# RG-LRU gates as half-row float32 products, both gates of a head side by side

## The chip, the cores and the metric

One core of a Trainium2 chip runs the whole program. The metric is device time in microseconds, from the first to the last instruction and what lies around them; lower is better. TensorE (PE) multiplies 128x128 stationary tiles with up to 512 moving columns into PSUM banks, ScalarE (ACT) evaluates functions, VectorE (DVE) does elementwise work and scans, GpSimd (POOL) does little here, and SyncE (SP) issues most DMAs.

## The reference

Two layers of a backbone over 256 latent tokens with a prefix of 256 context tokens, width 1024. Each layer has a token mixer with two branches (RG-LRU and HGRN2) and a ConvFFN. The change lies in the RG-LRU gates. There are 16 heads of 64 channels; each head has its own 64x64 matrix for each gate and direction:

```python
def rglru_coeffs(x, wa, ba, wx, bx, lam):
    xh = x.reshape(B, L, RG_HEADS, RG_HEAD_DIM)
    r = jax.nn.sigmoid(jnp.einsum('blhi,hij->blhj', xh, wa).reshape(B, L, D_RG) + ba)
    i = jax.nn.sigmoid(jnp.einsum('blhi,hij->blhj', xh, wx).reshape(B, L, D_RG) + bx)
    log_a = -RG_C * jax.nn.softplus(-lam) * r
    a = jnp.exp(log_a)
    b = jnp.sqrt(-jnp.expm1(2.0 * log_a)) * (i * x)
```

A linear scan h = a h + b follows, forwards and backwards, over context and then latents.

## The kernel before

Activations lie feature-major: 128 channels (a tile `t`, two heads) on the partitions, 512 tokens (256 latents, 256 context) in the columns. The big products are split: each float32 operand becomes a high and a low part (type fp32r), and `mm3` adds three products of the parts. `piece` makes the parts of the weights, `whi` on ACT (L221) and `wlo` on DVE (L222), into three buffers each; a new piece waits until PE has used an old one.

`rg_phase` runs once a layer. `PAT` gives its order: X is a group of the input projection whose rows feed the recurrence, F a group of the other rows, R a recurrence of two tiles (`recur`). There are four recurrences a layer. `gate_w` loads the gate matrices of a tile: it clears `gwr` on GpSimd (L552) and brings the two 64x64 blocks of a gate onto the diagonal of a 128x128 matrix, by four DMAs on SP (L555), for two gates and two directions. In layer 0 ACT and DVE split these (`gwh`, `gwl`, L562 and L563), and the input `xc` too (`xs`, L573 and L574); in layer 1 (`exact`) the products are full float32 without a split (L580). Each gate product has its own PSUM bank from `aux()`, four banks that the tag `ax` shares with all side products, and is read by one sigmoid (L583, which the profile shows at the helper's line L79).

After the sigmoids of two tiles come exp and tanh, a sqrt, two products and four scans of 256 tokens for each tile on DVE (L591 to L607), and L609 adds the directions. `r` and `q` (the tile `i[t]`) have two buffers each, so the first write of a recurrence's `q` waits for L609 of the recurrence before. Functions keep their order through `act`; a change of function set loads a table (ACT_TABLE_LOAD).

A scheduler fixes the order of the instructions on each engine when the kernel is built, from priorities and its own estimates of durations. At run time every engine takes its instructions strictly in that order.

Of the kernel before, what the change touches and what calls it, by code (L numbers as in the profile page):

```python
# [14 lines left out]
P = 128  # L15
# [12 lines left out]
# schedule of the start: a = a part of the conditioning, l / c = rows of latents / context, w = weights of a group,  # L28
# n = a pair of feature tiles normed and modulated, m = its products, s / t = per-channel columns
ORDER = 'laacwanaaawanasmnmmnmt'  # L30
# order of the RG phase per layer: X = a group of the recurrence's input, F = a group of the others, R = recurrence of two tiles
PAT = ['XFRXFRXFRXFFRFFF', 'XXRXFRXFRFFFRFFF']
# order of the HG phase per layer: V = values, C = block products of two heads, O = output gates, b / d = outputs, e = gating
HGO = ['VCObde', 'VCbd']
# pieces of conditioning per group of a main product: RG (second part), HG, merge and FFN of each layer
RATE = [0.9, 0.8, 0.8, 0.9, 0.1, 1.3, 1.0, 1.3]
# priorities of the chain from a product to the next layer's input, and of the split of weights
# [10 lines left out]
class Net:  # L48
# [28 lines left out]
    # functions of the activation tables keep their order of emission  # L77
# [66 lines left out]
    def columns_late(self, l):  # L144
# [7 lines left out]
        lam = t[:, 64:80]  # L152
        t = self.rows_to_cols([(m(I["ffn_conv_w"][l]), 66), (v(I["ffn_conv_b"][l]), 22), (v(I["g_pre_ffn"][l]), 8),
# [3 lines left out]
        # 8 * softplus(-lam) = 8 * (max(-lam, 0) + log1p(exp(-|lam|))), log1p(e) = 2 atanh(e / (2 + e))  # L157
# [51 lines left out]
    def piece(self, src, shape, pool=None):  # L209
# [5 lines left out]
        with self.tc.high_priority(offset=PRI):  # L215
            # short instructions where a chain of small ones runs beside them
# [14 lines left out]
    # columns [c0, c0+256) of w (1024 rows) as stationary; views: list of (psum slice, fn k -> (hi, lo))  # L231
# [16 lines left out]
    # a piece of side work after a group of the main product  # L248
# [8 lines left out]
    # all side work up to the last piece with this name  # L257
# [19 lines left out]
    # the same product with the vector engine: sums over the eight rows of each partition, ns streams  # L277
# [57 lines left out]
    # column groups of the tensor engine sum w columns each over the partitions, every sum 32 times  # L335
# [8 lines left out]
    # rows of steps: a step of each goes with the one before it of the next  # L344
# [36 lines left out]
    # 1 / sqrt(mean + eps) from the sums of both halves  # L381
# [14 lines left out]
    # rms norm of two token tiles of one stream, modulated, feature-major high and low parts  # L396
# [34 lines left out]
    # latents in column-major grid order after the context  # L431
# [15 lines left out]
    # y (two token tiles, psum halves): x + gate * rms_norm(y), kept in DRAM as well; then normed for the next layer  # L447
# [29 lines left out]
    # token-major product: acts (hi, lo) [128 k, ., tokens] stationary for two token tiles, w moving  # L477
    def tok_product(self, w, nk, act, psum):
# [13 lines left out]
        # the last three blocks go to one tile after the other, so that the first is done early  # L492
# [16 lines left out]
    def rg_phase(self, l, h, need_ctx, dr, first, more):  # L509
# [8 lines left out]
        exact = not need_ctx          # float32 gate products where the tensor engine has room  # L518
        with tc.tile_pool(name=self.nm("rg"), bufs=1, reuse_waits="tile") as pool:
            tl = lambda tag, n, w=512: lambda dt=F32: pool.tile([P, w], dt, tag=tag, name=self.nm(tag), bufs=n)  # L520
            XG, XS, SB = tl("xg", 18), tl("xs", 4), tl("sb", 2)
# [21 lines left out]
            def spill(dst, base):  # L543
# [4 lines left out]
                return ev  # L548

            def gate_w(t):  # L550
                raw = pool.tile([P, 4, P], F32, tag="gwr", name=self.nm("gwr"), bufs=2)
                nc.gpsimd.memset(raw, 0.0)  # L552
                for u in range(2):
                    for gi, nme in enumerate(("rg_wa", "rg_wx")):
                        nc.sync.dma_start(out=raw[u * 64:(u + 1) * 64, gi::2, u * 64:(u + 1) * 64],  # L555
                                          in_=I[nme][l, :, 2 * t + u].rearrange("d i j -> i d j"))
                if exact:
                    gw[t] = (raw, raw)
                    return
# [667 lines left out]
```

## Time and profile before

| | us |
|---|---|
| median of 3 runs (1780.99 to 1784.21) | 1782.84 |
| span of the profiled execution | 1778.8 |
| PE busy in the span | 1708.8 |
| DVE busy | 1277.1 |
| ACT busy | 914.6 |

The profile is of one execution. Its span runs from the first to the last instruction; the runs' times also hold what lies around it. The RG phase of layer 0 has its gates between about 70 and 180 us, that of layer 1 between about 1132 and 1225 us. A timeline row gives start, duration, engine, line, what was done and, in brackets, the idle time in front of it and what ended that. PE's durations overlap: neighbouring products start earlier than the one before has ended, so their pace is read from the starts. A full float32 product is shown as two matmuls.

### The profile page before, as it was taken

Reading aid. Unit: us, or ns where it says so; the run is one execution under the profiler, and the core shown is the slowest. Engines: PE = TensorE matmul, PEld = TensorE weight load, DVE = VectorE, ACT = ScalarE, POOL = GpSimd, SP = SyncE. Lnnn points to the kernel's source line nnn. Section 1 sums busy time; section 2 is a strip of 40 time slices with the busy share of each in tenths; the row PEclk is TensorE's granted clock in tenths of the full one; section 3 lists DMA queues with packets and bytes.
Section 4 is the critical chain, followed back from the end, with each engine's and each line's share of the span. In section 5 each row is a group of like instructions: output and inputs, shape, how many; then the busy total and the mean of one; then the engine's idle time right before and its main releaser. Section 6 shows DMA issues by size and latency. Waiting matters only on the chain.

```text
span 1778.8 us, 30752 instructions
## 1 busy us (share of the span) xinstructions
PE 1708.8 (96%) x12279; PEld 1414.7 (80%) x12279; DVE 1277.1 (72%) x2394; ACT 914.6 (51%) x1607; POOL 40.1 (2%) x65
## 2 busy tenths in 40 slices
PE   5999999999999999999999999999999999989998
PEld 3777877878877877877777878868997778969996
DVE  3788776788687887997766466686548877777764
ACT  4887732354444445533333354978444455656543
POOL 1000000000000000000000000000000000000000
PEclk9999999999999999999999999999999999989999
DMA  9422467524223167454544475233666323555563
GB/s 295 132 82 83 139 209 241 166 72 134 84 97 117 60 219 278 154 170 154 169 163 169 166 280 187 90 103 106 217 216 218 110 84 108 168 193 197 192 223 118
DMA packets 235291, 282.93 MB, mean 159 GB/s; under 512 B 18156, under 2 KB 211324, under 8 KB 235148
## 3 DMA queue, kind: packets, MB, share of 16 engines
q1 hardware_dynamic: 232156, 271.35, 46.1%
q10 hardware_dynamic: 2880, 9.51, 1.5%
q8 instruction: 96, 1.57, 0.4%
q14 instruction: 47, 0.39, 0.1%
q0 software_dynamic: 112, 0.11, 0.0%
HBM read 263.09 MB, written 17.85 MB: 158 GB/s over the span
## 4 chain that ended last, share of the span: by engine, by line
PE 78%; DVE 11%; ACT 5%; DMA 3%; issue 2%; POOL 1%; SPq 1%; DVEq 0%; POOLq 0%; ACTq 0%
PE mm L227 19%; PE mm L228 19%; PE mm L229 18%; PE mm L488 3%; PE mm L489 3%; PE mm L491 3%; DVE wlo L222 3%; DMA raw<-in_w_ada_dram 2%; PE ax L813 2%; PE ax L489 1%; PE ax L491 1%; PE ax L488 1%; ACT whi L221 1%; DVE q L607 1%; DVE q L605 1%
## 5 line engine op out<-in xcount | busy, mean ns | idle before, releaser
L227 PE MATMUL mm<-hi,whi 128*128 128x512 f32 (+1 forms) x1792 | 624.0, 349 | 2.2 <-DVE sb L678 1.4
L228 PE MATMUL mm<-lo,whi 128*128 128x512 f32 (+1 forms) x1792 | 620.8, 347 | 5.3 <-DVE lo L428 3.6
L229 PE MATMUL mm<-hi,wlo 128*128 128x512 f32 (+1 forms) x1792 | 618.5, 345 | 1.2 <-DVE wlo L222 1.1
L222 DVE TENSOR_TENSOR wlo<-raw,whi 128x1024 fp32r<-128x1024 f32 (+1 forms) x408 | 436.4, 1081 | 234.8 <-ACT whi L221 229.5
L221 ACT ACTIVATE whi<-raw 128x1024 fp32r<-128x1024 f32 (+1 forms) x408 | 378.9, 943 | 428.4 <-PE mm L228 245.4
L227 PEld LDWEIGHTS mm<-hi,whi 128*128 128x128 f32 x1792 | 337.6, 189 | 53.6 <-issue 5.5
L228 PEld LDWEIGHTS mm<-lo,whi 128*128 128x128 f32 x1792 | 337.3, 188 | 50.3 <-DVE lo L428 5.1
L229 PEld LDWEIGHTS mm<-hi,wlo 128*128 128x128 f32 x1792 | 337.0, 188 | 45.1 <-DVE wlo L222 2.0
L290 DVE SCALAR_TENSOR_TENSOR acc<-raw,s,acc 128x256 f32<-128x256 f32 x448 | 193.0, 479 | 2.1
L820 DVE TENSOR_TENSOR QK<-QK,T 128x1024 f32<-128x1024 f32 (+1 forms) x112 | 104.5, 955 | 13.2 <-PE ax L813 6.5
L829 ACT ACTIVATE kt<-QK 128x512 f32<-128x512 f32 (+1 forms) x80 | 45.1, 568 | 69.1 <-DVE QK L820 36.6
L228 PE MATMUL mm<-wlo,hi 128*128 128x256 f32 x256 | 72.3, 283 | 1.8 <-DVE wlo L222 1.8
L227 PE MATMUL mm<-whi,hi 128*128 128x256 f32 x256 | 72.8, 284 | 1.3 <-ACT whi L221 1.1
L229 PE MATMUL mm<-whi,lo 128*128 128x256 f32 x256 | 72.0, 281 | 0.0
L488 PE MATMUL mm<-whi,fh 128*128 128x512 f32 x176 | 68.9, 391 | 0.0
L489 PE MATMUL mm<-wlo,fh 128*128 128x512 f32 x176 | 68.7, 390 | 0.0
L393 POOL TENSOR_TENSOR rs<-ms,mhalf 128x1 f32<-128x1 f32 (+2 forms) x42 | 29.9, 712 | 1558.8 <-DVE ms L391 1558.8
L491 PE MATMUL mm<-whi,fl 128*128 128x512 f32 x176 | 54.9, 393 | 0.0
L227 PEld LDWEIGHTS mm<-whi,hi 128*128 128x128 f32 x256 | 48.6, 190 | 3.1 <-ACT whi L221 1.3
L228 PEld LDWEIGHTS mm<-wlo,hi 128*128 128x128 f32 x256 | 48.7, 190 | 2.5 <-DVE wlo L222 2.4
L229 PEld LDWEIGHTS mm<-whi,lo 128*128 128x128 f32 x256 | 48.7, 190 | 0.0
L79 ACT ACTIVATE acc<-acc 128x512 f32<-128x512 f32 (+1 forms) x44 | 22.6, 517 | 50.7 <-DVE acc L1034 50.6
(223 smaller groups left out, 2481.0 us busy)
## 6 DMA issues: line engine op xcount, KB each, us to landing
raw<-in_w_in_dram SPq DMA_DIRECT2D x72, 1024.0 KB
raw<-in_w_ada_dram SPq DMA_DIRECT2D x48, 1024.0 KB
raw<-in_ffn_w_up_dram SPq DMA_DIRECT2D x44, 1024.0 KB
raw<-in_ffn_w_down_dram SPq DMA_DIRECT2D x33, 1024.0 KB
raw<-in_w_out_dram SPq DMA_DIRECT2D x12, 1024.0 KB
raw<-in_w_proj_rg_dram SPq DMA_DIRECT2D x8, 1024.0 KB
raw<-in_w_proj_hg_dram SPq DMA_DIRECT2D x8, 1024.0 KB
xs<-xt SPq DMA_DIRECT2D x10, 512.0 KB
```

Of the source, the lines that this page charges most:

```text
L221: nc.scalar.activation(out=v(hi)[:, part, :], in_=src[:, part, :], func=AF.Copy)
L222: nc.vector.tensor_tensor(out=v(lo)[:, part, :], in0=src[:, part, :], in1=v(hi)[:, part, :], op=ALU.subtract)
L227: nc.tensor.matmul(out=out, lhsT=L[0], rhs=R[0], start=start, stop=False)
L228: nc.tensor.matmul(out=out, lhsT=L[0], rhs=R[1], start=False, stop=False)
L229: nc.tensor.matmul(out=out, lhsT=L[1], rhs=R[0], start=False, stop=stop)
L290: nc.vector.scalar_tensor_tensor(out=acc[:, st, :], in0=r3[:, k, :], scalar=s, in1=acc[:, st, :], op0=ALU.mult, op1=ALU.add)
L488: nc.tensor.matmul(out=out, lhsT=ah, rhs=hi[:, n, :], start=k == 0, stop=False)
L489: nc.tensor.matmul(out=out, lhsT=ah, rhs=lo[:, n, :], start=False, stop=False)
L491: nc.tensor.matmul(out=pss[i][n], lhsT=al, rhs=hi[:, n, :], start=False, stop=k == nk - 1)
L813: nc.tensor.matmul(out=o[32 * (b % 4):32 * (b % 4) + 32, b // 4 * 32:b // 4 * 32 + 32], lhsT=kt[:, b * 32:(b + 1) * 32], rhs=rhs(b), start ...
L820: nc.vector.tensor_tensor(out=u, in0=u, in1=sub(t, 1, [[-1, 2], [2, W // B], [0, B]]), op=ALU.mult)
L829: nc.scalar.activation(out=kt.rearrange("p (n h j) -> p n h j", h=2, j=B), in_=sub(qk, W, [[2 * B, W // (2 * B)], [W + B, 2], [1, B]]), fu ...
```

## The change

The gate matrices are no longer block-diagonal. For each tile and direction there is one 128x128 matrix `w[:, d, :]`: its upper 64 rows hold the first head's two gates side by side (`wa`, `wx`), its lower 64 rows the second head's (`wx`, `wa`). Two products with 64 rows each, one in either row half of the array, give one PSUM bank a head, with both gates in its 128 rows; both are full float32 in both layers. Each bank is read by two sigmoids of 64 partitions. For the gate `r` input and output lie on the same partitions; for `i` the sigmoid reads one half of the partitions and writes the other, with a bias that `bxs` holds swapped. So a tile and direction has two products and four sigmoids, where it had two products (three times two parts in layer 0) and two sigmoids. The clearing of `gwr` and the splits of gate matrices and of `xc` go; `gwr` has four buffers of half the size. The comments of the code are emptied too, which moves line numbers.

```diff
+        c["bxs"] = self.ct([P, 16], name="bxs")
+        for o in (0, 64):
+            nc.vector.tensor_copy(out=c["bxs"][o:o + 64, :], in_=c["bx"][64 - o:128 - o, :])
...
             def gate_w(t):
-                raw = pool.tile([P, 4, P], F32, tag="gwr", name=self.nm("gwr"), bufs=2)
-                nc.gpsimd.memset(raw, 0.0)
+                w = pool.tile([P, 2, P], F32, tag="gwr", name=self.nm("gwr"), bufs=4)
                 for u in range(2):
                     for gi, nme in enumerate(("rg_wa", "rg_wx")):
-                        nc.sync.dma_start(out=raw[u * 64:(u + 1) * 64, gi::2, u * 64:(u + 1) * 64],
+                        nc.sync.dma_start(out=w[u * 64:(u + 1) * 64, :, (gi ^ u) * 64:(gi ^ u) * 64 + 64],
                                           in_=I[nme][l, :, 2 * t + u].rearrange("d i j -> i d j"))
-                if exact:
-                    gw[t] = (raw, raw)
-                    return
-                wh = pool.tile([P, 4, P], F32R, tag="gwh", name=self.nm("gwh"), bufs=2)
-                wl = pool.tile([P, 4, P], F32R, tag="gwl", name=self.nm("gwl"), bufs=2)
-                nc.scalar.activation(out=wh, in_=raw, func=AF.Copy)
-                nc.vector.tensor_tensor(out=wl, in0=raw, in1=wh, op=ALU.subtract)
-                gw[t] = (wh, wl)
+                gw[t] = w
...
-                    if not exact:
-                        xh, xl = XS(F32R), XS(F32R)
-                        nc.scalar.activation(out=xh, in_=xr, func=AF.Copy)
-                        nc.vector.tensor_tensor(out=xl, in0=xr, in1=xh, op=ALU.subtract)
                     r[t], i[t] = R(), Q()
                     for d in range(2):
-                        for gi, bn, o in ((0, "ba", r[t]), (1, "bx", i[t])):
-                            ps = self.aux()
-                            if exact:
-                                nc.tensor.matmul(out=ps, lhsT=wh[:, 2 * d + gi, :], rhs=xr, start=True, stop=True)
-                            else:
-                                self.mm3(ps, (wh[:, 2 * d + gi, :], wl[:, 2 * d + gi, :]), (xh, xl), True, True)
-                            self.act(out=o[:, d, :], in_=ps, func=AF.Sigmoid, bias=C[bn][:, d * 8 + t:d * 8 + t + 1])
+                        pss = [self.aux() for _ in range(2)]
+                        for ps, hv in zip(pss, halves):
+                            nc.tensor.matmul(out=ps, lhsT=w[hv, d, :], rhs=xc[t][hv, :], start=True, stop=True,
+                                             tile_position=(hv.start, 0))
+                        c = slice(d * 8 + t, d * 8 + t + 1)
+                        for u, hv in enumerate(halves):
+                            self.act(out=r[t][hv, d, :], in_=pss[u][hv, :], func=AF.Sigmoid, bias=C["ba"][hv, c])
+                        for u, hv in enumerate(halves):
+                            other = halves[1 - u]
+                            self.act(out=i[t][hv, d, :], in_=pss[u][other, :], func=AF.Sigmoid, bias=C["bxs"][other, c])
```

The scheduler lays the instructions out anew. Three places follow, with the order of before first.

PE, first recurrence of layer 0. `ax` is a bank of the gates, `mm` one of the main products; L227 to L229 are the three products of `mm3`.

```order
164 L228 MATMUL mm_742<-lo_81,whi_734 128x512
165 L227 MATMUL ax_622<-xs_616,gwh_588 128x512
166 L228 MATMUL ax_622<-xs_617,gwh_588 128x512
167 L227 MATMUL ax_627<-xs_616,gwh_588 128x512
168 L229 MATMUL ax_622<-xs_616,gwl_589 128x512
169 L228 MATMUL ax_627<-xs_617,gwh_588 128x512
170 L229 MATMUL ax_627<-xs_616,gwl_589 128x512
```

```order
159 L232 MATMUL mm_709<-hi_80,wlo_702 128x512
160 L571 MATMUL ax_611<-xg_595,gwr_585 128x512
161 L571 MATMUL ax_612<-xg_595,gwr_585 128x512
162 L571 MATMUL ax_619<-xg_595,gwr_585 128x512
163 L571 MATMUL ax_620<-xg_595,gwr_585 128x512
164 L230 MATMUL mm_709<-hi_80,whi_701 128x512
165 L231 MATMUL mm_709<-lo_81,whi_701 128x512
166 L232 MATMUL mm_709<-hi_80,wlo_702 128x512
167 L230 MATMUL mm_709<-hi_80,whi_701 128x512
168 L571 MATMUL ax_629<-xg_600,gwr_590 128x512
169 L571 MATMUL ax_630<-xg_600,gwr_590 128x512
```

The 24 gate products of two tiles stood in two blocks of twelve; the eight halves now stand as four, two and two, with main products between them, and five places earlier among the main products.

PE, fourth recurrence of layer 1. `mm` is here a product of the HGRN2 values, 256 columns wide.

```order
5240 L229 MATMUL mm_11238<-whi_11182,lo_9681 128x256
5241 L580 MATMUL ax_11295<-xg_10881,gwr_11036 128x512
5242 L580 MATMUL ax_11298<-xg_10881,gwr_11036 128x512
5243 L580 MATMUL ax_11301<-xg_10881,gwr_11036 128x512
5244 L580 MATMUL ax_11306<-xg_10911,gwr_11042 128x512
5245 L580 MATMUL ax_11309<-xg_10911,gwr_11042 128x512
5246 L580 MATMUL ax_11312<-xg_10911,gwr_11042 128x512
5247 L580 MATMUL ax_11315<-xg_10911,gwr_11042 128x512
5248 L227 MATMUL mm_11356<-whi_11348,hi_9680 128x256
```

```order
5267 L230 MATMUL mm_11334<-whi_11278,hi_9582 128x256
5268 L231 MATMUL mm_11334<-wlo_11279,hi_9582 128x256
5269 L571 MATMUL ax_11228<-xg_10823,gwr_10961 128x512
5270 L232 MATMUL mm_11334<-whi_11278,lo_9583 128x256
5271 L230 MATMUL mm_11334<-whi_11278,hi_9582 128x256
5272 L231 MATMUL mm_11334<-wlo_11279,hi_9582 128x256
5273 L232 MATMUL mm_11334<-whi_11278,lo_9583 128x256
5274 L230 MATMUL mm_11334<-whi_11278,hi_9582 128x256
5275 L571 MATMUL ax_11229<-xg_10823,gwr_10961 128x512
```

Seven gates stood in a row, 96 main products behind the first. Now four halves come first, 89 main products follow, and the other four halves stand singly with five, seven and six main products between them.

ACT, second recurrence of layer 1. `r` and `q` are the outputs of the sigmoids of the two gates, `a` that of the exp.

```order
826 L79 ACTIVATE r_10778<-ax_10780,cols_816 128x512
827 L79 ACTIVATE q_10779<-ax_10783,cols_816 128x512
828 L79 ACTIVATE r_10778<-ax_10786,cols_816 128x512
829 L79 ACTIVATE q_10779<-ax_10789,cols_816 128x512
830 L79 ACTIVATE r_10792<-ax_10794,cols_816 128x512
831 L79 ACTIVATE q_10793<-ax_10797,cols_816 128x512
```

```order
850 L79 ACTIVATE r_10684<-ax_10686,cols_783 64x512
851 L79 ACTIVATE r_10684<-ax_10687,cols_783 64x512
852 L224 ACTIVATE whi_10834<-raw_10828 128x1024
853 L79 ACTIVATE q_10685<-ax_10686,bxs_785 64x512
854 L79 ACTIVATE q_10685<-ax_10687,bxs_785 64x512
855 L79 ACTIVATE r_10684<-ax_10694,cols_783 64x512
856 L79 ACTIVATE r_10684<-ax_10695,cols_783 64x512
857 L79 ACTIVATE q_10685<-ax_10694,bxs_785 64x512
858 L79 ACTIVATE q_10685<-ax_10695,bxs_785 64x512
859 L79 ACTIVATE r_10702<-ax_10704,cols_783 64x512
```

Eight sigmoids of 128 partitions have become sixteen of 64, and a bank is handed back only after the `q` sigmoid of its pair.

## Rows read from the trace of the kernel before

**Rows 1.** The page: the span, and PE's busy time, share and instructions.

```profile
span 1778.8 us, 30752 instructions
PE 1708.8 (96%) x12279; PEld 1414.7 (80%) x12279; DVE 1277.1 (72%) x2394; ACT 914.6 (51%) x1607; POOL 40.1 (2%) x65
```

**Rows 2.** Stretches: length, busy us (count) of PE, PEld, DVE, ACT, POOL; clock, DMA.

```profile
60.00:180.00 120.00, 115.52 (x493) 91.37 (x492) 94.27 (x165) 93.35 (x128) 3.15 (x6) 1.00 0.28 85
1132.00:1225.00 93.00, 89.71 (x494) 68.33 (x493) 72.49 (x87) 77.61 (x104) 3.15 (x6) 1.00 0.34 105
```

**Rows 3.** Timeline of ACT, layer 1: the first `q` sigmoid of three recurrences.

```profile
1162.46 0.69 ACT L79 ACTIVATE q<-ax,cols 128x512 f32<-128x512 f32 x1 [2.70 <-DVE xg L609]
...
1188.25 0.69 ACT L79 ACTIVATE q<-ax,cols 128x512 f32<-128x512 f32 x1 [2.73 <-DVE xg L609]
...
1216.57 0.69 ACT L79 ACTIVATE q<-ax,cols 128x512 f32<-128x512 f32 x1 [0.87 <-DVE xg L609]
```

**Rows 4.** Timeline of DVE, layer 1: first and last step of a tile.

```profile
1178.47 1.23 DVE L595 SCALAR_TENSOR_TENSOR r<-a,r 128x1024 f32<-128x1024 f32 x1 [2.14 <-ACT r L79]
...
1187.74 0.42 DVE L609 TENSOR_TENSOR xg<-q 128x256 f32<-128x256 f32 x1
```

**Rows 5.** PE's waits, 60 to 180 and 1132 to 1262 us: total, times, longest.

```profile
PE ax L228 <- DVE xs L574: 2.6, 2, 1.5
PE ax L227 <- DVE cols L133: 1.1, 1, 1.1
PE ax L227 <- ACT gwh L562: 0.8, 1, 0.8
...
PE ax L580 <- ACT q L79: 2.2, 2, 1.1
PE mm L228 <- DVE wlo L222: 1.8, 2, 1.1
PE mm L227 <- ACT whi L221: 1.1, 1, 1.1
PE ax L580 <- issue: 1.0, 2, 0.5
```

**Rows 6.** Timeline of PE around a sum over partitions in column groups.

```profile
240.83 0.39 PE L228 MATMUL mm<-lo,whi 128*128 128x512 f32 x1
241.06 0.40 PE L229 MATMUL mm<-hi,wlo 128*128 128x512 f32 x1
241.39 0.42 PE L340 MATMUL ax<-acc,ones 128*32 128x128 f32 x8
```

**Rows 7.** Timeline of PE in layer 1, from the first gates on.

```profile
1132.75 3.67 PE L580 MATMUL ax<-xg,gwr 128*128 128x512 f32 x8 [0.49 <-issue]
...
1136.49 3.59 PE L580 MATMUL ax<-xg,gwr 128*128 128x512 f32 x8
...
1219.59 0.68 PE L227 MATMUL mm<-whi,hi 128*128 128x256 f32 x1
...
1228.83 0.28 PE L227 MATMUL mm<-whi,hi 128*128 128x256 f32 x1
...
1232.60 0.28 PE L229 MATMUL mm<-whi,lo 128*128 128x256 f32 x1
```

**Rows 8.** Timeline of PE: eight float32 products of the conditioning, four column groups.

```profile
15.23 1.94 PE L271 MATMUL ax<-raw,s 128*32 128x256 f32 x16
```

**Rows 9.** Timeline of ACT: sigmoids of the first recurrence of layer 1.

```profile
1135.21 0.69 ACT L79 ACTIVATE r<-ax,cols 128x512 f32<-128x512 f32 x1
...
1136.37 0.69 ACT L79 ACTIVATE r<-ax,cols 128x512 f32<-128x512 f32 x1
1136.94 0.70 ACT L79 ACTIVATE q<-ax,cols 128x512 f32<-128x512 f32 x1
```

**Rows 10.** Line 562, a copy that goes: count, ns, first and last start.

```profile
L562 ACT ACTIVATE gwh<-gwr x8: 614/616/630, 71.4 to 154.4; 128x512 fp32r<-128x512 f32 x8
```

**Rows 11.** The chain of waits, 66 to 73 us: the first gate weights' last DMA.

```profile
67.56 3.74 DMA gwr<-in_rg_wx_dram
```

More of the change, by code (lines that the diff above doesn't have):

```diff
@@ L517, in rg_phase @@
         ys = {}
-        exact = not need_ctx
         with tc.tile_pool(name=self.nm("rg"), bufs=1, reuse_waits="tile") as pool:
             tl = lambda tag, n, w=512: lambda dt=F32: pool.tile([P, w], dt, tag=tag, name=self.nm(tag), bufs=n)
-            XG, XS, SB = tl("xg", 18), tl("xs", 4), tl("sb", 2)
+            XG, SB = tl("xg", 18), tl("sb", 2)
             t2 = lambda tag, n: lambda: pool.tile([P, 2, 512], F32, tag=tag, name=self.nm(tag), bufs=n)
@@ L564, in gate_w @@
-                gw[t] = (wh, wl)
+                gw[t] = w
             def recur(ts):
                 r, i, a = {}, {}, {}
+                halves = (slice(0, 64), slice(64, P))
                 for t in ts:
-                    wh, wl = gw.pop(t)
-                    xr = xc[t]
-                    if not exact:
-                        xh, xl = XS(F32R), XS(F32R)
-                        nc.scalar.activation(out=xh, in_=xr, func=AF.Copy)
-                        nc.vector.tensor_tensor(out=xl, in0=xr, in1=xh, op=ALU.subtract)
+                    w = gw.pop(t)
```

## The prediction

> **What bounds the kernel now.** I read the page first: TensorE (PE) is busy for 1708.8 of the 1778.8 us span [rows 1], so PE is the bound of the kernel as a whole, and microseconds taken from it count where nothing else ends last. The change touches only the two stretches in which the recurrence gates are computed, so the table by stretches comes next [rows 2]: 60 to 180 us (layer 0) and 1132 to 1225 us (layer 1). PE fills 115.5 of 120 and 89.7 of 93 there. The reader should look at ScalarE (ACT) beside it: 93.4 of 120, but 77.6 of 93, which leaves 15.4 us in layer 1.
>
> Then the timelines, to see what ends a wait. A recurrence of two tiles is a loop over three engines: sigmoids on ACT, exp, tanh and sqrt on ACT, the scans on VectorE (DVE), and the next recurrence's `q` sigmoid can start only when the sum at L609 has released the buffer of `q`. ACT waits for exactly that: 2.70 us at 1162.46, 2.73 at 1188.25, 0.87 at 1216.57 [rows 3]. From the first sqrt's end at 1178.47 to L609's end at 1188.16 DVE runs almost without a gap [rows 4]. So in layer 1 this loop, with a period of 25.8 and then 28.3 us, is nearly as long as PE's work beside it, and two of PE's waits there are for a `q` sigmoid to hand back a bank [rows 5]. Both are tight, and a change that shortens one and lengthens the other is to be worked out on both.
>
> **PE work.** A split product of 512 columns starts every 0.23 us (240.83, 241.06 [rows 6]), one of 256 columns every 0.118 us (32 between 1228.83 and 1232.60 [rows 7]). A full float32 product shows as two passes; eight of them (four gates) and one split product lie between 1132.75 and 1136.49, so a pass is (3.74 - 0.23) / 8 = 0.44 us [rows 7]. Layer 0 gives up 32 x 3 x 0.232 = 22.3 us and layer 1 gives up 32 x 0.88 = 28.2 us. Each layer gets 32 half-row float32 products of two passes.
>
> What a half costs isn't in the trace; no product there uses half the rows. Upper bound: nothing overlaps, 0.88 each, 28.2 a layer. Lower bound: the two halves of a pair run side by side, 0.88 a pair, 14.1 a layer. The nearest row is the conditioning product: eight float32 products in four column groups, sixteen passes of 256 columns, in 1.94 us [rows 8]. One such pass alone would take 0.22, so serial is 3.5 us and full overlap 0.9. What fits is that the second pass of one product lies beside the first pass of the next, which gives 9 slots x 0.22 = 1.98. I take that: a run of n neighbouring halves costs n + 1 passes. By the order, the runs are 4, 2, 2 in six recurrences, 3, 1, 2, 2 in the second of layer 0 and 4, 1, 1, 1, 1 in the last of layer 1. Layer 0: (11 + 12 + 11 + 11) x 0.44 = 19.8, **-2.5 us**. Layer 1: (33 + 13) x 0.44 = 20.2, **-8.0 us**.
>
> The Trainium skill (TensorE: Matmul & The Clock Gate, section "Part 3: Packing small matmuls") says that matmuls in different row groups run concurrently, a few ns apart. By that a pair would be one product, the lower bound above; the conditioning row shows about half of the overlap that this would give.
>
> **Waits that go.** In layer 0 PE waits 2.6 + 1.1 + 0.8 = 4.5 us for the copies and splits in front of gates [rows 5]; those on `xs` and `gwh` go with the instructions, the one on `cols` stood just ahead of gates that now stand elsewhere. In layer 1 it is 2.2 + 1.0 around the gates, and 1.1 + about 1.1 at a weight piece that ACT had queued behind a sqrt [rows 5]; the order now puts that piece between the sigmoids, so I count about 5 us. The memsets on GpSimd and DVE's splits go too; nothing on the path waited for the first, and the second shorten DVE in layer 0.
>
> **ACT work.** Sigmoids start 0.57 us apart (1136.37, 1136.94) [rows 9]. A half has as many columns as a whole one, so I take the same 0.57; from a quarter less (fewer partitions) to a quarter more, since no row shows a half. There are 32 more a layer: +18.2 us. Layer 0 gives back 16 copies of 0.62 [rows 10], 8 of L562 and 8 of L573, net +8.3, and has 26.6 us to spare. Layer 1 gives nothing back and has 15.4.
>
> **New waits on PE.** There are four `ax` banks. A pair holds two until all four of its sigmoids are through: 4 x 0.57 = 2.28 us, where a whole gate held one for 0.57. The third pair of a recurrence therefore can't start before the first pair's third sigmoid, nor the fourth before the second's. Everything behind such a half in PE's order, the main products first of all, waits too.
>
> Layer 1, from the order and the rows. First recurrence: sixteen sigmoids from 1135.21 end at 1144.3, not 1140.8: 3.5 us late. Before the first sqrt the order now puts three weight pieces instead of one and two evacuations instead of one, 2.4 us more; that makes 5.9, of which DVE, with two weight pieces fewer between its steps, takes back 2.0: 3.9 us late at the release of `q`. The second turn of the loop takes 25.8 now; eight more sigmoids add 4.6 and one more weight piece about 0.6: 31.0. The third takes 28.3 now and some 29.4 then, because ACT stands still for part of the 28.3 and the sigmoids fill that. So the releases come at 1166.4, 1197.4 and 1226.8, which is 3.9, 9.1 and 10.2 us later than 1162.46, 1188.25 and 1216.57. PE doesn't stand still for that long, since the order has moved main products in front of the late halves: 31 instead of 5 in the second recurrence (6.0 us more), 112 instead of 10 in the third, and 89 between the first four halves and the rest in the fourth. Its waits come to about 1.0, 2.9, 3.1 and 3.9 us. For the last: the third gates wait for the sigmoid at 1226.8, and with the main products between the single halves the last one ends at 1233.2. The same place among the main products, 107 behind the start of the fourth recurrence's gates, is passed at 1219.6 + 107 x 0.118 = 1232.2 now [rows 7], with 2.2 us of waits right behind it, so 1234.4. **Layer 1: -1.2 us.** It hardly matters here what a half costs: PE waits for the loop in any case.
>
> Layer 0, by the same rule: 1.3 us for the gate weights, which land at 71.3 (issue at 67.56 plus 3.74 [rows 11]) while the halves now stand five products earlier in the order, then 0.4, 2.5, 2.6 and 1.5 us for banks in the four recurrences, 8.3 in all. -2.5 - 4.5 + 8.3 = **+1.3 us**.
>
> The Trainium skill (TensorEngine Tiling (Array Packing), section "PSUM Bottleneck") says that tiling speeds up TensorE and not the evacuation behind it. It speaks against this change, and the ACT rows here agree.
>
> **The sum.** -1.2 + 1.3 = +0.1 us on the profiled execution, whose span is 1778.8; the median of the runs is 1782.84, 4.0 us above it, which lies around the span and stays. I forecast **1782.9 us**, no change that can be told: a measurement of this kernel tells 0.2%, 3.6 us.
>
> **Rivals.**
> *ACT becomes the bound of layer 1 (slower).* In that stretch 77.6 us of ACT work, 18.2 of new sigmoids and the waits for L609 that ACT can't use (0.87 + 2.73 + 2.70 in [rows 3], and three like them of 1.0 to 2.8) make 102 to 108 us against 93, 9 to 15 too many. Against it: evacuations and weight pieces can slide behind the last gates, where ACT has room. Each microsecond by which the fourth release comes after 1228 goes to the end. With up to two thirds of it sliding, +4 to +13: 1787 to 1796.
> *The halves don't overlap (slower or none).* PE gets 28.2 instead of 19.8 in layer 0, part of it inside waits it would have anyway: +1.5 to +8.4, so 1784 to 1791. For it: no row shows row halves. Against: column groups do overlap.
> *PE stays the bound (faster).* If ACT hands the banks back as early as the planner of the order assumes, half of the 19.2 us of new waits (10.9 and 8.3) is gone: 1773; all of it, 1764. With full overlap of the halves on top (0.05 of this rival's 0.19) PE's work falls by another 9.2, 1754 at best; with the banks' waits as I have them most of those 9.2 us would only lengthen the waits. Against it: ACT's waits for L609.
> *The change doesn't do what it says:* the row halves could force a pause of the array at each run. The column groups of a sum over partitions start 0.33 us after the product ahead of them instead of 0.23 [rows 6]; 0.1 us for each of 27 runs (13 and 14) would be +2.7, inside the range.
>
> **How the numbers follow.** Forecast 0.46 (its own range 1778 to 1788, mostly within 0.2%), ACT-bound 0.23, no overlap 0.12, PE-bound 0.19. The range takes in the near half of the ACT-bound case and the first half of the PE-bound one: 1772 to 1793. Faster: 0.19 and a sliver of the forecast, 0.21. Slower: 0.23, half of the no-overlap case and a tenth of the forecast, 0.32. Same: 0.47.
>
> **What would show it.** Half-row passes whose starts overlap within a pair; sigmoids on 64 partitions 0.57 apart; `q` sigmoids of layer 1's second to fourth recurrence 4, 9 and 10 us later against their gates' start; PE waits under "ACT q" of 2 to 4 us each, where there were two of 1.1. I am wrong if these waits stay near 1 us (then PE's saving arrives), if halves have a shorter pace on ACT, or if weight pieces start to stop PE after the gates of layer 1.

## The result: 0.94% slower, and the profile after

The changed kernel takes 1803.36 us (median of four executions, 1795.27 to 1804.85). The kernel before, beside it on the same chip, takes 1781.91. The ratio is 1.0094 with a 95% interval of 1.0070 to 1.0118. The forecast was 1782.9 with a range of 1772 to 1793, so the time lies 10 us above the range.

The profiled execution has a span of 1800.4 us, 21.6 above the 1778.8 of [rows 1]. The page of the changed kernel:

```profile
span 1800.4 us, 30675 instructions
PE 1727.4 (96%) x12247; PEld 1408.3 (78%) x12247; DVE 1268.1 (70%) x2382; ACT 952.4 (53%) x1655; POOL 32.0 (2%) x49
...
L571 PE MATMUL ax<-xg,gwr 64*128 64x512 f32 x128 | 53.4, 730 | 15.9 <-ACT q L79 12.4 <-DVE cols L133 2.3 <-DMA gwr<-in_rg_wx_dram 0.8
```

PE is busy for 18.6 us *longer* than in [rows 1] although its gate work was cut. The last line is the group of the row halves: 15.9 us of waiting in front of them, 12.4 of it for a `q` sigmoid to free a bank.

To find where the 21.6 us arise I compare the same step in both traces, a small power on GpSimd that each norm does (line 393 before, 396 after):

| place | before | after | later by |
|---|---|---|---|
| behind layer 0's recurrences | 387.08 | 395.79 | 8.7 |
| ahead of layer 1's | 1110.17 | 1118.92 | 8.8 |
| behind layer 1's | 1392.10 | 1409.72 | 17.6 |
| last FFN, start | 1585.19 | 1603.88 | 18.7 |
| last norm | 1773.13 | 1795.04 | 21.9 |

So layer 0's recurrences cost 8.7 us and layer 1's 8.9 (290.8 from norm to norm, 281.9 before); the rest comes behind. What the stretches look like, before and then after (columns: length, busy us and count of PE, PEld, DVE, ACT, POOL, then the granted TensorE clock and the DMA share):

```profile
60.00:252.00 192.00, 187.52 (x807) 149.06 (x806) 149.12 (x258) 132.99 (x182) 3.15 (x6) 1.00 0.36 117
1104.00:1300.00 196.00, 186.51 (x1276) 162.89 (x1275) 133.82 (x191) 142.50 (x222) 5.78 (x11) 0.98 0.42 136
```

```profile
60.00:252.00 192.00, 185.25 (x731) 133.00 (x730) 131.14 (x224) 144.86 (x195) 0.00 (x0) 0.96 0.35 111
1104.00:1300.00 196.00, 180.09 (x1153) 150.05 (x1152) 131.15 (x198) 161.08 (x256) 2.29 (x4) 0.93 0.38 123
```

PE's idle time grew by 2.3 us (4.5 to 6.8) in the first stretch and by 6.4 (9.5 to 15.9) in the second. The larger part is in the column of the clock. Here are the places where it isn't 1.00 in the changed kernel:

```profile
104.00:116.00 12.00, 9.72 (x32) 5.70 (x31) 11.57 (x49) 8.73 (x13) 0.00 (x0) 0.86 0.27 80
142.00:154.00 12.00, 10.59 (x26) 6.10 (x27) 8.57 (x12) 10.57 (x16) 0.00 (x0) 0.72 0.27 89
176.00:188.00 12.00, 10.47 (x27) 5.20 (x26) 5.64 (x8) 11.72 (x17) 0.00 (x0) 0.72 0.06 23
1174.00:1186.00 12.00, 9.86 (x25) 5.02 (x26) 7.27 (x10) 9.72 (x15) 0.00 (x0) 0.72 0.31 97
1194.00:1204.00 10.00, 8.37 (x59) 8.40 (x60) 7.24 (x9) 8.72 (x12) 0.00 (x0) 0.83 0.27 84
1237.00:1259.00 22.00, 17.71 (x51) 11.03 (x52) 14.24 (x23) 14.94 (x21) 0.00 (x0) 0.61 0.14 48
```

Length times (1 - clock) is the time that TensorE lost by running at the lower of its two levels, 1.2 in place of 2.4 GHz. PE is busy throughout these falls (17.07 of 17.07 us in the longest, 1241.39 to 1258.46), so that time is lost in full. The rows give 1.7 + 3.4 + 3.4 = 8.4 us in layer 0 and 3.4 + 1.7 + 8.6 = 13.7 in layer 1, where the kernel before lost 0 and 3.4. One of these places in PE's timeline (start, duration, engine, line, operation, shapes, wait ahead and its releaser):

```profile
141.18 0.40 PE L231 MATMUL mm<-lo,whi 128*128 128x512 f32 x1
143.41 1.83 PE L571 MATMUL ax<-xg,gwr 64*128 64x512 f32 x4 [1.83 <-ACT q L79]
145.17 0.50 PE L232 MATMUL mm<-hi,wlo 128*128 128x512 f32 x1
...
149.52 0.63 PE L230 MATMUL mm<-hi,whi 128*128 128x512 f32 x1
149.95 0.63 PE L231 MATMUL mm<-lo,whi 128*128 128x512 f32 x1
```

PE waits 1.83 us for a bank, and from 145.7 to 152.5 the granted clock is at its lower level. The main products that follow start 0.43 us apart (149.52, 149.95), not 0.23 as in [rows 6]; they have nothing to do with the gates and pay all the same.

With that a balance can be drawn. It has to run from norm to norm, over the same work in both traces; behind the two stretches PE waits 1.3 and 1.8 us less than before, so its idle time grows by 1.0 us up to the norm behind layer 0 (5.85 to 6.84, from 70 us on) and by 4.6 in layer 1 (12.71 to 17.30). Layer 0: +1.0 of idle time and +8.4 of clock make +9.4, and 8.7 were measured, which leaves 0.7 that the lighter products gave back; I had said 2.5. Layer 1: +4.6 and +10.3 make +14.9, and 8.9 were measured, which leaves 6.0; I had said 8.0. Such a rest is good to some 2.5 us: between the layers, where nothing was changed and the length is the same (723.1 us), PE's idle time comes out 2.5 us lower (12.05 and 9.59) and its busy time as much higher. Of what comes behind layer 1, 1.7 us are clock as well: the dip at the start of the last FFN, which both kernels have, is longer here (0.83 between 1610 and 1620 us). That part isn't surely the change's, since the last FFN varies by itself: the kernel before with a third buffer for `q` (below) needed 7.8 us more than the kernel before from its start to the last norm in one execution and 0.2 more in another.

### The profile page after: what moved, and what is told of

Read it like the earlier page. It is cut to its first block, busy times and chain, and to the rows that moved or that the text cites. A ratio compares the mean times of both kernels' runs of the same rounds, so it can differ in the third digit from the quotient of the medians.

```text
span 1800.4 us, 30675 instructions
## 1 busy us (share of the span) xinstructions
PE 1727.4 (96%) x12247; PEld 1408.3 (78%) x12247; DVE 1268.1 (70%) x2382; ACT 952.4 (53%) x1655; POOL 32.0 (2%) x49
## 4 chain that ended last, share of the span: by engine, by line
PE 76%; DVE 10%; ACT 8%; DMA 3%; issue 2%; POOL 1%; SPq 1%; DVEq 0%; POOLq 0%; ACTq 0%
PE mm L230 18%; PE mm L231 18%; PE mm L232 18%; PE mm L491 3%; PE mm L492 3%; PE mm L494 3%; DVE wlo L225 2%; ACT r L79 2%; DMA raw<-in_w_ada_dram 2%; PE ax L808 2%; ACT whi L224 1%; PE ax L571 1%; ACT q L79 1%; PE ax L492 1%; PE ax L494 1%
## 5 line engine op out<-in xcount | busy, mean ns | idle before, releaser
L571 PE MATMUL ax<-xg,gwr 64*128 64x512 f32 x128 | 53.4, 730 | 15.9 <-ACT q L79 12.4
```

What stands on the lines that cost most here:

```text
L571: nc.tensor.matmul(out=ps, lhsT=w[hv, d, :], rhs=xc[t][hv, :], start=True, stop=True, tile_position=(hv.start, 0))
```

## The theories

The trace says that the clock is the loss, and not why it falls. Each of these six falls stands behind a wait of PE of 1.5 us or more, and products on half of the rows lie beside it. Two theories: **(1)** the waits alone lower the clock; the extra sigmoids make the waits, and the half rows are harmless. **(2)** The half rows do it, alone or together with waits. A third question is which part of the change is to blame for the time at all, the row halves or the half sigmoids.

## Experiments

**One layer at a time.** The other layer keeps the gate code of the kernel before. This is layer 0 alone; layer 1 alone has `not need_ctx` in the first line:

```diff
+        rows = need_ctx
...
+                if rows:
                     for t in ts:
                         w = gw.pop(t)
...
+                else:
+                    for t in ts:
+                        wh, wl = gw.pop(t)
```

> Row halves and half sigmoids in layer 0 alone, layer 1's gates as in the kernel before. In the trace of the changed kernel the same norms stand 8.7 us later than before when layer 0's recurrences are over (387.08 against 395.79), and 7.3 to 8.8 us later when layer 1 begins. If the layers add up, this kernel is 7 to 9 us above the kernel before: 1789 to 1791, with the granted clock at half for about 17 us between 100 and 190 us and at full level in layer 1's recurrences. If layer 1's loss came from what layer 0 hands over and not from its own gates, this kernel would lose about 18 to 21 us: 1800 to 1803.

> Row halves and half sigmoids in layer 1 alone, layer 0's gates as in the kernel before. In the changed kernel layer 1's recurrences add 8.9 us (norms at 1110.17 and 1118.92, then at 1392.10 and 1409.72) and the end of the kernel 4.2 more. If the layers add up: 9 to 13 us above the kernel before, 1791 to 1795, with the clock at half in some 27 us of layer 1's recurrences. If only the two layers together do it: within 4 us of the kernel before.

Measured: layer 0 alone 1.0036 (1.0017 to 1.0055), some 6 us; layer 1 alone 1.0073 (1.0049 to 1.0097), some 13. Together 1.09% against 0.94%: the layers add up, and each loses by itself. Layer 0 alone lost 5.0 us of clock in its own stretch, less than the 8.5 that go with the 17 us at half clock that I expected; layer 1 alone lost 13.6 in its own and none in layer 0.

Layer 1 alone also shows that beside half rows no wait of 1.5 us is needed. Two of its falls stand behind a wait of 1.05 us at 1135.8 and behind two of 0.74 and 0.44 us at 1200.4 and 1201.5, with half products right behind them:

```profile
1134.00:1146.00 12.00, 10.95 (x28) 6.19 (x27) 6.55 (x8) 11.71 (x17) 0.00 (x0) 0.72 0.16 40
1196.00:1212.00 16.00, 14.82 (x81) 11.19 (x80) 11.73 (x16) 14.49 (x22) 0.00 (x0) 0.79 0.30 103
```

**Row halves with whole sigmoids.**

```diff
-    for u, hv in enumerate(halves):
-        self.act(out=r[t][hv, d, :], in_=pss[u][hv, :], func=AF.Sigmoid, bias=C["ba"][hv, c])
-    for u, hv in enumerate(halves):
-        other = halves[1 - u]
-        self.act(out=i[t][hv, d, :], in_=pss[u][other, :], func=AF.Sigmoid, bias=C["bxs"][other, c])
+    for ps, bn, o in ((pss[0], "ba", r[t]), (pss[1], "bx", i[t])):
+        self.act(out=o[:, d, :], in_=ps, func=AF.Sigmoid, bias=C[bn][:, c])
```

> The changed kernel with whole sigmoids: the 128 partitions of the first bank of a pair go to r, those of the second to i, so the two gates of every second head change places and the values are other ones; the row halves stay, ScalarE has 32 sigmoids fewer a layer, and a bank is free after one sigmoid. Theory 1 (the waits for banks lower the clock, the row halves are harmless to it): PE's waits of 1.5 us and more at the gates go, the granted clock stays at 1.00 in both stretches up to the dip of the kernel before, and PE's saving arrives: 10 to 19 us below the kernel before, 1763 to 1772. Theory 2 (products on half of the rows lower the clock by themselves): the clock is at half in most of the places where it is now, some 20 us are lost to it, and the time is 1785 to 1795.

Measured: 0.9997 (0.9978 to 1.0015), in neither theory's range. The whole loss goes with the 32 extra sigmoids a layer; but the gain of theory 1 doesn't come. Waits stay: three of 1.5 us in layer 0, 1.4 and 2.5 in layer 1. One at 1182 us is followed by a fall, the others are not:

```profile
128.00:140.00 12.00, 9.95 (x37) 5.81 (x34) 10.78 (x14) 7.87 (x12) 0.00 (x0) 1.00 0.17 60
...
1180.00:1196.00 16.00, 13.10 (x55) 9.95 (x56) 14.16 (x19) 9.22 (x13) 0.00 (x0) 0.68 0.20 66
```

The balance from norm to norm: layer 0 is 1.4 us shorter (385.73 for 387.08) with 0.1 less idle time and no clock lost, so the products gave 1.3. Layer 1 is 0.5 us longer with +3.2 of idle time and +5.1 of clock (one more fall of 1.7 us stands at 1362), so they gave 7.8. So row halves alone don't lower the clock as a rule, and without the half sigmoids the change would gain nothing that can be told.

**Full rows in place of row halves.** The banks and the half sigmoids stay; each head's 64 rows of weights are filled up with zeros:

```diff
-    nc.tensor.matmul(out=ps, lhsT=w[hv, d, :], rhs=xc[t][hv, :], start=True, stop=True, tile_position=(hv.start, 0))
+    nc.tensor.matmul(out=ps, lhsT=w[:, 2 * u + d, :], rhs=xc[t], start=True, stop=True)
```

> The changed kernel with full rows: each product has its 64 rows of weights filled up with 64 rows of zeros and runs over all 128 rows, so that nothing of a pair can overlap; banks, sigmoids and results stay. Theory 1 (the waits lower the clock): the clock falls behind the same waits, for about as long, and PE has 16 passes x 0.44 = 7 to 8 us more work a layer, some of it inside the waits: 1804 to 1820. Theory 2 (the half rows lower the clock): the clock stays at 1.00 behind waits of the same length, 20 us of the loss go and up to 15 us of passes come: 1790 to 1800.

Measured: 1.0046 (1.0028 to 1.0063), half of the changed kernel's loss, with *more* work for PE. The same places among the products:

```profile
104.00:116.00 12.00, 10.57 (x40) 6.95 (x38) 11.68 (x47) 8.01 (x11) 0.53 (x1) 1.00 0.19 59
142.00:154.00 12.00, 10.85 (x39) 6.89 (x39) 9.32 (x13) 11.46 (x17) 0.00 (x0) 1.00 0.28 89
176.00:188.00 12.00, 11.24 (x41) 7.21 (x40) 5.87 (x8) 11.33 (x17) 0.00 (x0) 1.00 0.01 1
1172.00:1184.00 12.00, 10.65 (x50) 7.65 (x51) 7.34 (x11) 11.22 (x16) 0.53 (x1) 1.00 0.33 100
1190.00:1200.00 10.00, 8.56 (x73) 8.25 (x73) 8.06 (x9) 9.95 (x15) 0.00 (x0) 1.00 0.27 91
1232.00:1254.00 22.00, 19.25 (x118) 16.05 (x117) 14.36 (x23) 17.12 (x25) 0.00 (x0) 0.84 0.21 66
```

The clock stays at 1.00 at five of six places. That speaks for theory 2. But PE, with more to do, also waits less: 4.3 us in the first stretch and 13.2 in the second, 2.8 at most, where the changed kernel has 6.8, 15.9 and 4.4. What can be compared are the short waits: four of 1.1 to 1.4 us at or near the gates (108, 144, 1173 and 1192 us) stand in places of this table whose clock is 1.00, where those of 1.05 and 0.74 us in layer 1 alone, beside half rows, were followed by a fall (and the three of 1.5 us with whole sigmoids were not). For the long waits the two causes aren't apart yet.

**Half sigmoids alone.** The kernel before, each sigmoid cut in two:

```diff
-    self.act(out=o[:, d, :], in_=ps, func=AF.Sigmoid, bias=C[bn][:, d * 8 + t:d * 8 + t + 1])
+    for hv in (slice(0, 64), slice(64, P)):
+        self.act(out=o[hv, d, :], in_=ps[hv, :], func=AF.Sigmoid,
+                 bias=C[bn][hv, d * 8 + t:d * 8 + t + 1])
```

> The kernel before with each gate's sigmoid cut into two of 64 partitions: ScalarE gets the sigmoids of the changed kernel (64 a layer at some 0.71 us, where 32 stood at 0.57, so +27 us a layer), PE keeps its products on all rows, and a bank is held for 1.42 us. Theory A (a wait lowers the clock only where products on half of the rows lie beside it): PE waits 4 to 8 us more in both layers together, the granted clock stays as in the kernel before, 4 to 8 us above it (ratio 1.002 to 1.005). Theory B (the longer waits lower the clock whatever the products): waits of 1.5 us and more at the gates are followed by half clock, 10 to 20 us go to that, 14 to 26 us above the kernel before (ratio 1.008 to 1.015).

Measured: 1.0133 (1.0106 to 1.0159), *worse* than the whole change. That is theory B's time, but not its way: neither theory had the place. The longest of PE's waits in layer 0 (waited for, total, times, longest):

```profile
PE mm L227 <- ACT xg L540: 10.7, 2, 6.7
```

Here ScalarE still has the copies of [rows 10] as well, and it comes so late that the *main* products have no bank: 6.7 and 4.0 us. The norm behind layer 0 comes 18.7 us later. Both waits have a fall beside them although every product uses all rows; these two rows hold 5.0 us of lost clock, part of it while PE still waited:

```profile
99.00:111.00 12.00, 5.33 (x17) 3.93 (x16) 10.20 (x18) 8.39 (x11) 0.53 (x1) 0.72 0.32 101
144.00:152.00 8.00, 4.18 (x11) 2.84 (x12) 7.48 (x9) 5.42 (x8) 0.00 (x0) 0.79 0.48 150
```

In layer 1 two waits, 2.4 us at 1252 and 1.9 at 1207, are not followed by a fall (the clock is 1.00 over the whole stretch): waits as long as those of the changed kernel, all rows in use, no loss.

**Full rows, longer waits.** The full-row kernel with every sigmoid of `r` done twice:

```diff
+    for _ in range(2):
         self.act(out=r[t][hv, d, :], in_=pss[u][hv, :], func=AF.Sigmoid, bias=C["ba"][hv, c])
```

> The full-row kernel (64 rows of zeros beside each head's weights, same banks as the changed kernel) with every sigmoid of r done twice: 32 half sigmoids more a layer at 0.71 us, +23 us of ScalarE, so that PE waits at the gates at least as long as in the changed kernel (over 12 us in all, single ones over 2 us). Theory A (half rows beside a wait are what lowers the clock so often): mean granted clock still at 0.991 or more, under 8 us lost in the two stretches, though the waits are longer. Theory B (only the length of the waits counts): 15 us or more lost in the two stretches, mean clock 0.988 or less. The time is above the full-row kernel in both cases, by some 10 to 30 us, from the waits.

Measured: 1.0177 (1.0148 to 1.0207). The long waits came, three of them in layer 1: 2.7 us at 1233, 4.2 at 1268, 5.3 at 1297 (in layer 0 they didn't: 4.0 us of idle time in all). What stands around them:

```profile
1230.00:1240.00 10.00, 7.33 (x39) 5.89 (x38) 6.68 (x10) 9.67 (x16) 0.00 (x0) 0.83 0.41 131
1262.00:1274.00 12.00, 7.83 (x42) 5.62 (x41) 11.93 (x18) 10.87 (x17) 0.00 (x0) 0.86 0.37 124
1290.00:1304.00 14.00, 8.70 (x57) 8.50 (x56) 11.21 (x15) 13.26 (x23) 0.00 (x0) 0.76 0.37 127
```

Each wait is followed by lost clock, 1.7, 1.7 and 3.4 us of it. In the changed kernel the wait of 4.38 us at 1241 lost 8.6. So with full rows a long wait does lower the clock, as it did in layer 0 of the half-sigmoid kernel, and here the clock is back after 3.4 to 6.8 us. The profiled stretches stayed under the 8 us of theory A; the mean clock over all executions, 0.9898, fell between the two. This is where I end: the runs speak for waits and half rows acting together, and give no rule for it.

**The same kernel again.**

> The changed kernel unaltered, beside the others of this group. If the clock's falls belong to the kernel and not to one execution: mean granted clock of 0.983 to 0.988 over all executions (the kernel before 0.993), falls at the long waits beside half rows again, though not all at the same ones, and a ratio of 1.007 to 1.012 to the kernel before. If they were chance: a clock near 0.993 and a ratio under 1.004.

Measured: 1.0103 (1.0070 to 1.0135), mean clock 0.9853 over four executions against 0.9933 for the kernel before. The falls again, in this execution:

```profile
108.00:120.00 12.00, 9.81 (x25) 5.96 (x26) 11.33 (x48) 8.54 (x13) 0.00 (x0) 0.72 0.33 100
146.00:158.00 12.00, 10.71 (x28) 5.74 (x29) 8.45 (x11) 10.09 (x16) 0.00 (x0) 0.72 0.27 89
1176.00:1188.00 12.00, 9.81 (x25) 5.03 (x26) 7.28 (x10) 9.76 (x15) 0.00 (x0) 0.72 0.30 96
1194.00:1206.00 12.00, 10.12 (x66) 8.85 (x65) 9.03 (x10) 10.63 (x15) 0.00 (x0) 0.86 0.31 101
1238.00:1262.00 24.00, 20.02 (x72) 13.13 (x71) 15.27 (x24) 16.75 (x23) 0.00 (x0) 0.64 0.15 50
```

Five of the six places return. The third of layer 0 doesn't (a wait of 1.53 us at 182, as long as before, without a fall), so a single wait may or may not be followed by one; the sum is the kernel's, not the execution's.

**A third buffer for `q`**, in the changed kernel and in the kernel before:

```diff
-            R, Q, A = t2("r", 2), t2("q", 2), t2("a", 2)
+            R, Q, A = t2("r", 2), t2("q", 3), t2("a", 2)
```

> The changed kernel with three buffers for q in place of two, so that a q sigmoid need not wait for the sum of the recurrence before it. Theory A (it is the loop over q that makes PE wait, and the wait beside half rows that lowers the clock): the waits for a q sigmoid in layer 1 fall from 8.7 us to under 3, the 13.7 us of clock lost there to under 5, and the time comes 10 to 16 us below the changed kernel (ratio to the kernel before 1.000 to 1.004). Theory C (ScalarE's work, not the loop, is what PE waits for): the sigmoids come as late as now, and the time stays within 4 us of the changed kernel (1.007 to 1.012).

> The kernel before with three buffers for q, nothing else: what the third buffer is worth where sigmoids are whole. PE waits 2.2 us there for a q sigmoid (two waits of 1.1). If these go and nothing is late behind them: 2 to 4 us below the kernel before (ratio 0.998 to 0.999). If VectorE's chain sets the loop anyway: no change.

Measured: the changed kernel 1.0054 (1.0033 to 1.0074), between the two theories. The waits for `q` sigmoids in layer 1 fall only from 8.7 to 6.9 us, so ScalarE's work is late even where the loop doesn't hold it back; yet the clock lost there falls from 13.7 to 3.4 us. The kernel before with the buffer: 0.9983 (0.9964 to 1.0001), and in more rounds:

> The kernel before with a third buffer for q, in more rounds: it measured 0.9983 with an interval that just reached 1. In layer 1 its trace gained 7.9 us. If that gain is the buffer's: ratio 0.996 to 0.999 with an interval below 1. If it was chance: 0.999 to 1.001.

Measured: 0.9964 (0.9947 to 0.9980), faster than both kernels. Its waits of PE in layer 1, all of them:

```profile
PE mm L228 <- DVE lo L428: 2.6, 2, 1.6
PE mm L228 <- DVE wlo L222: 2.0, 2, 1.7
PE ax L419 <- DVE xh L405: 1.7, 2, 1.5
```

The 2.2 us for `q` and the 1.0 of issue in [rows 5] are gone, no clock is lost in the stretch, and layer 1's recurrences take 6.8 us less (1384.08 - 1108.92 = 275.2 against 281.9).

**Full float32 in layer 0 without row halves**, alone and with the buffer:

```diff
-        exact = not need_ctx
+        exact = True
```

> The kernel before with full float32 gate products in layer 0 too, on all rows with zeros, without the copies and splits: what layer 0's precision change does without row halves and without half sigmoids. PE's gate products 28.2 instead of 22.3 us (+5.9), the waits for xs and gwh (3.4 us) go, ScalarE loses 10 us of copies: +1 to +4 us (ratio 1.0005 to 1.002). If the waits for the splits stood for more than they show, 0 to -3 us.

> The kernel before with full float32 gates on all rows in layer 0 too and a third buffer for q. The first alone measured 1.0008, the second 0.9983; if both add up, 0.999, if ScalarE's 10 us less in layer 0 help only together with the buffer, 0.996 to 0.998.

Measured: 1.0008 (0.9988 to 1.0027), inside the expected range and no difference that can be told; with the buffer 0.9968 (0.9948 to 0.9987), which is the buffer's gain alone.

The mean granted clock over all executions of each kernel puts the main runs in one line:

| kernel | rows | sigmoids | executions | mean clock | ratio |
|---|---|---|---|---|---|
| before | all | whole | 72 | 0.993 | 1 |
| float32 in both layers | all | whole | 10 | 0.993 | 1.0008 |
| row halves, whole sigmoids | half | whole | 10 | 0.991 | 0.9997 |
| full rows | all | half | 10 | 0.994 | 1.0046 |
| full rows, `r` sigmoids twice | all | half | 4 | 0.990 | 1.0177 |
| changed, three `q` | half | half | 10 | 0.988 | 1.0054 |
| changed | half | half | 8 | 0.985 | 1.0094, 1.0103 |
| half sigmoids alone | all | half | 4 | 0.989 | 1.0133 |

A mean clock that is 0.01 lower stands for 18 us of a span of 1800. The changed kernel loses (0.993 - 0.985) x 1800 = 14 us that way, of the 17 to 18 that its ratios stand for. "Full rows" keeps the changed kernel's sigmoids and the clock of the kernel before, and half of the loss is gone. Four rows of the table are the corners of a square of rows and sigmoids: with whole sigmoids the row halves change nothing that can be told (1.0008 and 0.9997; the first has a bank for each gate, not for each head), with half sigmoids they cost another 0.5% (1.0046 against 1.0094 and 1.0103).

## Why the prediction was wrong, step by step

**What bounds the kernel.** Right as far as it went: PE bounds, ScalarE's loop over `q` is tight beside it. But the table that I read [rows 2] has the clock in it, 1.00 in both stretches, and I took that for a constant. The trace of the kernel before already showed otherwise, some 8 and 15 us outside the stretch of layer 1 that I read:

```profile
1111.00:1117.00 6.00, 4.97 (x27) 4.77 (x28) 4.24 (x8) 4.01 (x8) 0.65 (x2) 0.72 0.41 133
1233.00:1240.00 7.00, 4.92 (x28) 4.72 (x29) 6.95 (x8) 6.97 (x14) 0.00 (x0) 0.76 0.42 127
```

The second row has two waits of 1.1 us within 2 us of each other, and the products behind them start 0.21 us apart in place of the 0.118 of [rows 7]. I had counted these two waits as time that goes and not asked what they did to the products behind.

**The sum, which is the step that failed.** "-1.2 + 1.3 = +0.1 us" had terms for products, for waits that go and for waits that come, and none for the pace of the main products behind a wait. That term is +8.4 us in layer 0 and +10.3 in layer 1, 18.7 of the 21.6. The other terms came near to what I said, the sigmoids apart, which cost half as much again:

- *PE work.* -2.5 and -8.0 said, -0.7 and -6.0 left by the balance (-1.3 and -7.8 with whole sigmoids), which is as near as such a rest can tell. Its working was off in two ways that pull against each other. The halves overlap fully, not as "n + 1 passes": the first passes of a pair start within 0.01 us of each other (first row, of 114.70 to 114.74 us alone), a run of two takes 1.06 us (1.32 said), a run of four 1.92 (2.2 said):

```profile
114.72 0.70 PE L571 MATMUL ax<-xg,gwr 64*128 64x512 f32 x2
...
114.72 1.13 PE L571 MATMUL ax<-xg,gwr 64*128 64x512 f32 x4
115.78 0.50 PE L230 MATMUL mm<-hi,whi 128*128 128x512 f32 x1
116.11 0.40 PE L231 MATMUL mm<-lo,whi 128*128 128x512 f32 x1
...
174.09 1.99 PE L571 MATMUL ax<-xg,gwr 64*128 64x512 f32 x8
176.01 0.50 PE L230 MATMUL mm<-hi,whi 128*128 128x512 f32 x1
```

  Two products on full rows, from the full-row kernel:

```profile
177.55 1.96 PE L572 MATMUL ax<-xg,gwr 128*128 128x512 f32 x4 [0.65 <-issue]
178.94 0.80 PE L232 MATMUL mm<-hi,wlo 128*128 128x512 f32 x1
179.58 0.40 PE L230 MATMUL mm<-hi,whi 128*128 128x512 f32 x1
```

  The product behind them starts on record 1.39 us later, but on top of their last pass, and the next one 0.64 us after it, not 0.23. Up to that second product behind, two take 2.03 us on full rows and 1.39 as halves (114.72 to 116.11). On the other side a pair behind a full bank takes 1.76 (143.41 to 145.17), since its second half waits for a bank of its own inside the pair. The rival "the halves don't overlap" is refuted. The Trainium skill (TensorE: Matmul & The Clock Gate, section "Part 3: Packing small matmuls") says that row groups run side by side, and the starts of a pair within 0.01 us agree with it; my row of column groups did not.
- *New waits on PE.* 8.3 said for layer 0 and 6.8 measured: 3.7 for banks, 0.8 for the gate weights and 2.3 for `cols`, which I had not expected there. 10.9 said for layer 1 and 11.0 measured (8.7 for `q`, 1.9 for `xg`, 0.4 issue). The waits in the changed kernel, layer 1:

```profile
PE ax L571 <- ACT q L79: 8.7, 5, 4.4
...
PE mm L230 <- DVE xg L536: 1.9, 1, 1.9
```

- *Waits that go.* Those for `xs`, `gwh` and the weight piece behind the fourth recurrence's gates went; the one for `cols`, 1.1 before, which I had let go, is the 2.3.
- *ACT work.* A half sigmoid takes 0.71 us, not 0.57: at the far end of the bound that I gave. That is 64 x 0.71 - 32 x 0.57 = 27.2 us a layer in place of 18.2. So the loop turned slower than I said: the first `q` sigmoids of the second, third and fourth recurrence come 32.8, 67.7 and 97.9 us after the first sigmoid of layer 1, where the prediction's releases stand at 31.2, 62.2 and 91.6. The first rows are the pace, the last is the fourth recurrence:

```profile
1142.61 1.39 ACT L79 ACTIVATE r<-ax,cols 64x512 f32<-64x512 f32 x2
1144.03 1.39 ACT L79 ACTIVATE q<-ax,bxs 64x512 f32<-64x512 f32 x2
...
1240.55 0.68 ACT L79 ACTIVATE q<-ax,bxs 64x512 f32<-64x512 f32 x1 [3.12 <-DVE xg L604]
```

**The rivals.** "ACT becomes the bound of layer 1" had the right side and the nearest time, 1787 to 1796. The full-row kernel, which has its sigmoids and little of the clock's loss, lies in that range (1.0046, some 1790), but only in part by its cause: 5.4 us come in layer 0, where full rows give PE more to do and its idle time falls by 1.0, and 1.8 in layer 1. It was too small for the same reason as the forecast, and it lacked layer 0, which the half sigmoids cost as much. "PE stays the bound" fell: even with whole sigmoids the saving goes into new waits and the clock behind them. The Trainium skill's remark on evacuation (TensorEngine Tiling (Array Packing), section "PSUM Bottleneck"), which I had weighed, that tiling doesn't speed up what empties the banks, held: with row halves the runs with whole and with half sigmoids differ by 1% of the kernel.

**What would show it.** The signs that I named came (starts that overlap, waits of 2 to 4 us under `q`, later `q` sigmoids). They were signs of a mechanism whose waits I had priced about right; its larger cost, the slower products behind the waits, had no sign among them.

What stays open: how a wait and half rows act together on the clock. The mean clocks speak for the two together doing more than each alone (0.993 with neither, 0.994 and 0.991 with one, 0.985 with both). But PE waits less on full rows, and the run that made those waits longer did so in layer 1 only and lies between, at 0.990. Which wait will be followed by a fall isn't shown: the same wait of 1.53 us was followed by one in one execution and not in the other, in layer 1 alone a wait of 1.05 us was, and in the changed kernel with three buffers two waits of 2.5 and 2.6 us were not.

## What to carry to other kernels

A wait on TensorE can cost its own length and the slower products behind it, here more in these than in itself: read the clock column behind each wait of the trace, and add a term for it before summing. Count what a packing of small products does to the engine that empties their banks: here 32 more evacuations a layer cost 1% beside row halves (0.4% on full rows, 1.0046 against 1.0008), and the packed products gave 7 to 9 us of 1780 by the balances. Where a loop over engines is tight, one more buffer (0.9964 here) can do more than cheaper products.

## What the runs showed of the hardware that I had not expected

- A sigmoid over 64 partitions and 512 columns is *slower* than one over 128: the starts lie 0.71 us apart, not 0.57, while the duration of one is the same (683 and 687 ns on average). It is so with shifted partitions and without, and also where both halves read one bank (pairs start 1.40 us apart in the half-sigmoid kernel, 1153.67 and 1155.07).
- Two float32 products on the two row halves start within 0.01 us of each other. Up to the second product behind them two take 1.39 us and four 2.26 (174.09 to 176.35); on all rows two take 2.03 and four 3.67 (172.13 to 175.80 in the full-row kernel).
- Behind a wait of 4.4 us with single halves among the products the granted clock stayed at its lower level from 1241.4 to 1258.5 us (changed kernel); behind one of 4.2 us with full products it was back after some 3 us (full rows, `r` sigmoids twice).
